# Second FFN's up projection by seven block products instead of eight (Strassen's scheme), with two of four weight sums made by accumulating DMAs

## Chip, core and metric

The kernel runs on one core of one Trainium2 chip. The metric is the device time of one launch in microseconds (us).

## What is computed

A decoder trunk of two layers works on 512 tokens of 1024 features in float32. Each layer adds a gated mixer (attention in layer 0, a state space layer beside a gated delta rule in layer 1) and then a gated convolutional feed-forward network (FFN). The change is in the second layer's FFN:

```python
def conv_ffn(h, w_up, conv_w, w_down):        # h 512 x 1024, w_up 1024 x 5632, w_down 2816 x 1024
    up = causal_dwconv(h @ w_up, conv_w)      # three taps over the tokens
    a, b = jnp.split(up, 2, axis=-1)          # 2816 columns each
    return (jax.nn.silu(a) * b) @ w_down
```

## The kernel before

Features lie on the 128 partitions and tokens on the free axis. Every float32 operand of a large product is split in two float32r tiles, the rounded value and the rest (`whi`, `wlo` for weights, `hh`, `hl` for activations), and a product of two operands is three matmuls: hi by hi, hi by lo, lo by hi (`mm3`, lines 324 to 326). One output tile of 128 features and 512 tokens takes eight feature blocks of the input, so 24 matmuls of 512 columns (`gemm`). A new stationary operand is loaded for every matmul.

`ffn` runs over `NJ` = 22 pairs of up-projection tiles, `j` for the half that passes through silu and `NJ + j` for the other. For pairs 0 and 1 (taken together, by halves of 256 tokens, right behind the norm) and then one pair at a time, it makes both products and calls `finish`: `conv` scales the accumulator on ScalarE (line 520) and adds two shifted copies on VectorE (lines 521, 522), for `a` and for `b`; then come silu (line 527), the product (line 529) and the split into `gh` and `gl` (lines 343, 344). Behind pairs 8 and 15 the down projection of the third that is complete is made (eight tiles, 24 or 21 matmuls each), and behind pair 21 the last third, in `out_gemm`.

Weights come by `prep`: SyncE loads a 128x1024 tile `st` of 512 KB, ScalarE rounds it (`whi`, line 312) and VectorE takes the rest (`wlo`, line 313). `weight` prepares `LA` = 2 tiles ahead. `st` has 2 buffers, `whi` and `wlo` have 5. The accumulators rotate over six PSUM banks named acc, s and o. `make_h` writes the normed activations: a scaled copy `hu` (line 474), then `hh` (line 475) and `hl` (line 476), by halves of 256 tokens. The order in which an engine meets its instructions is set at build time by a scheduler that goes by priorities, so instructions of neighbouring pairs interleave on each engine, while each engine works strictly through its own queue.

Of the kernel before, what the change touches and what calls it, by code (L numbers as in the profile page):

```python
# [8 lines left out]
F32 = mybir.dt.float32  # L9
F32R = mybir.dt.float32r  # L10
# [6 lines left out]
P = 128  # L17
T = 512
# [53 lines left out]
# features of the state space layer: groups of 16 (o) for states of odd and even tiles of states  # L72
# [3 lines left out]
def place(g):  # L76
    """Place of a group of 16 features among the eight of a half."""
    return 4 * (g // 2 % 2) + 2 * (g // 4) + g % 2
# [111 lines left out]
def weight_order():  # L190
    o = [("q", c, p) for p in range(2) for c in range(3)]
    o += [("q", c, p) for c in range(3, 9) for p in range(2)]
    o += [("wo", m) for m in range(8)]

    def ffn(l):
        r = []
        for j in range(NJ):
            r += [("up", l, j), ("up", l, NJ + j)]
            if j in THIRDS[1:3]:
                r += [("dn", l, THIRDS.index(j) - 1, m) for m in range(8)]  # L200
        return r + [("dn", l, 2, m) for m in range(8)]

    o += ffn(0)
    o += [("ri", 0), ("ri", 1), ("ab",)]
    kq = lambda p: [("ri", 8 + 2 * p), ("ri", 2 + 2 * p), ("ri", 9 + 2 * p), ("ri", 3 + 2 * p)]
    need = {"k": kq, "v": lambda p: [("ri", 14 + 2 * p), ("ri", 15 + 2 * p)], "z": lambda p: [("z", p, 0), ("z", p, 1)]}
    for e in SEQ.split():
        if e[0] in need:
            o += need[e[0]](int(e[1]))
    o += [("ro", m) for m in range(8)]  # L210
    o += ffn(1)
    return o
# [17 lines left out]
SPLIT_AT = (18, 18, 18, 18)  # L230
REC_K = (2, 3, 4, 5, 0, 1, 6, 7)


class Kernel:
    def __init__(self, nc, tc, I, O, ctx):
        self.nc, self.tc, self.I, self.O, self.ctx = nc, tc, I, O, ctx
        self.guards = {}
        self.cst = self.open("cst")
        self.wp = self.open("wp")
        self.sp = self.open("sp")  # L240
        self.ps = ctx.enter_context(tc.tile_pool(name="ps", bufs=1, space=PSUM))
        self.order = weight_order()
        self.index = {k: n for n, k in enumerate(self.order)}
        self.next = 0
        self.ready = {}
        self.LA = 2
        self.turn = 0
        self.tturn = 0

# [48 lines left out]

    def prep(self, pool=None, stage=None):
        key = self.order[self.next]  # L300
        self.next += 1
        src, n = self.source(key)
        nc = self.nc
        wp = pool or self.wp
        if stage:
            st = stage[0].tile([P, 1024], F32, name="ast", tag=stage[1], bufs=stage[2])[:, :n]
        else:
            st = wp.tile([P, 1024], F32, name="st", tag="st", bufs=1 if pool else 2)[:, :n]
        nc.sync.dma_start(st, src)
        hi = wp.tile([P, 1024], F32R, name="whi", tag="whi", bufs=1 if pool else 5)[:, :n]  # L310
        lo = wp.tile([P, 1024], F32R, name="wlo", tag="wlo", bufs=1 if pool else 5)[:, :n]
        nc.scalar.copy(hi, st)  # L312
        nc.vector.tensor_tensor(lo, st, hi.bitcast(F32), ALU.subtract)  # L313
        self.ready[key] = (hi, lo)

    def weight(self, key):
        ix = self.index[key]
        while self.next < min(ix + (self.LA if ix > 5 else 0) + 1, len(self.order)):
            self.prep()
        return self.ready.pop(key)  # L320
# [39 lines left out]
    def ada_first(self, k, pool, V):  # L360
        """Scale and shift of a feature tile of the first norm, in three steps: loads, long sums, last sums."""
# [11 lines left out]
        if k in ADA_PE:  # L373
            # four parts of the sum side by side on the tensor engine
# [67 lines left out]
    def rstd_bc(self, stats, cs, tag="x", warm=None):  # L442
        """1 / rms of each token, on all partitions; stats: squares to be summed."""
# [26 lines left out]
    def make_h(self, l, kind, k, rs, cs):  # L470
        nc = self.nc
        u = self.sp.tile([P, T], F32, name="hu", tag="hu", bufs=2)[:, cs]
        hi, lo = (t[:, cs] for t in self.h[k])
        nc.vector.scalar_tensor_tensor(u, self.x[k][:, cs], self.scale(l, kind, k), rs[:, cs], ALU.mult, ALU.mult)
        nc.scalar.activation(hi, u, AF.Identity, bias=self.shift(l, kind, k))  # L475
        self.last = nc.vector.scalar_tensor_tensor(lo, u, self.shift(l, kind, k), hi.bitcast(F32), ALU.add, ALU.subtract)  # L476
# [6 lines left out]
    def out_gemm(self, keys, rhs, gates, l, kind, hpool=None, order=None, tags=("acc", "acc", "s", "s", "o", "o", "acc", "acc")):  # L483
        """Products that end a half layer, with the norm that follows; the last tiles go by halves of the tokens."""
# [3 lines left out]
        for m0 in range(0, 4, 2):  # L488
            # the first two tiles leave the operand that comes last to the end
# [20 lines left out]
    def ffn(self, l, after, hpool=None):  # L510
        nc, tc = self.nc, self.tc
        lo, hi = slice(0, 256), slice(256, T)
        gp, tp = self.open(f"fg{l}", "right"), self.open(f"ft{l}", "right")
        if True:
            G = {}

            def conv(acc, c, tag):
                t = tp.tile([P, T], F32, name="t" + tag, tag="t" + tag, bufs=2)
# [18 lines left out]
            for j in range(NJ):  # L537
                if j < 2:
# [28 lines left out]
    def attention(self):  # L567
# [4 lines left out]
        if True:  # L572
# [13 lines left out]
            def rmsn(srcs, n):  # L586
                """Each head of both banks divided by its rms; srcs: [P, 2, n * 64] each."""
# [50 lines left out]
            def scores(pair, i, qT, kT, bias, isA):  # L638
                """Scores, softmax with its maximum, and division, for one block of queries of two heads."""
# [62 lines left out]
            # entry: modulation, norm and the first chunks together, feature tile by feature tile  # L702
# [3 lines left out]
            def keep_warm(n, k=0):  # L706
                """Products that nobody reads, to bring the tensor engine to its full clock and to keep it there."""
# [122 lines left out]
        # the turn of a state in two parts, the first short enough to be multiplied exactly  # L830
# [24 lines left out]
        # half angles keep the argument well inside the function's range  # L855
# [17 lines left out]
        # (l - 1) / lambda  # L873
# [67 lines left out]
    def s5_inputs(self):  # L941
        """W1, turned so that tokens and features of a chunk lie on the partitions."""
# [21 lines left out]
    def recurrent(self):  # L964
# [8 lines left out]
        # projections of u and of the decay and write rates; the first tiles by halves of the tokens  # L973
# [7 lines left out]
        # tokens of u by their place in a chunk  # L981
# [26 lines left out]
        # running sums of g with tokens on the free axis, rounded and rest on their own partitions, each chunk in its own columns  # L1008
# [70 lines left out]
        def decays(h):  # L1079
            """Of a head: exp(G) of every token, and exp(G_i - G_j) for the pairs of a chunk."""  # L1080
# [10 lines left out]
        def keys_queries(h, p):  # L1091
            """k and q of a head: decays, k's norm, and the two masked and decayed products with k."""
# [38 lines left out]
        def diagonal(p):  # L1131
            """Inverses of the 16 x 16 unit triangles on the diagonal, one to a partition, by substitution."""
# [29 lines left out]
        def block(flat, b):  # L1162
            """The 32 x 32 blocks b on the diagonals of all eight triangles, rows first."""
# [3 lines left out]
        def levels(p):  # L1167
            """Doubles the blocks of the inverses X and of their transposes W: the new block is -X22 N21 X11."""
# [8 lines left out]
            # 16 -> 32  # L1177
# [17 lines left out]
            # 32 -> 64  # L1195
# [18 lines left out]
            # 64 -> 128  # L1214
# [68 lines left out]
        def s5_load(f):  # L1283
            """What half of the features and of the states needs, the features' tokens by their place in a chunk."""
# [12 lines left out]
        def s5_states(f):  # L1297
            """States at the chunks' ends: the turn taken out, a real recurrence, the turn put back."""
# [31 lines left out]
        def s5_tokens(f):  # L1330
            """Outputs from the chunk's own tokens and from the state before it."""
# [21 lines left out]
        def s5_out():  # L1353
# [7 lines left out]
            for m in range(2):  # L1361
# [3 lines left out]
                # twice the gated output: 2 sigmoid(x) = 1 + tanh(x / 2), of the same table as gelu  # L1365
# [61 lines left out]
        hC = self.open("hC", "right")  # L1427
        self.out_gemm([("ro", m) for m in range(8)], rhs, lambda m: self.gate(1, 0, m), 1, 1, hC, REC_K, ("acc", "acc", "t", "x", "s", "s", "o", "o"))
# [91 lines left out]
```

## Time and profile before

| | |
|---|---|
| Runs of the kernel | 1324.92, 1325.09, 1325.41 us, median 1325.09 |
| Profiled execution: span from first to last instruction | 1321.6 us |
| Profiled execution: its own time | not recorded beside the span; the median of the runs is 3.5 us above the span |
| PE busy in the span | 1302.3 us (99%) |
| VectorE busy | 910.8 us (69%) |
| ScalarE busy | 576.0 us (44%) |
| Granted TensorE clock | 1.000 of full speed, mean |
| Matmuls | 8190 |

The profile names the engines PE (matmuls), PEld (loads of the stationary operand), DVE (VectorE), ACT (ScalarE), POOL (GpSimd) and SP (SyncE). A matmul's recorded duration overlaps its neighbours', and so does a VectorE instruction's; the distance from one start to the next tells what an engine can do. Times in a timeline count from the span's start. The second FFN's up projection begins at about 954 us with pairs 0 and 1.

### The profile page before, as it was taken

Reading aid. Unit: us, or ns where it says so; the run is one execution under the profiler, and the core shown is the slowest. Engines: PE = TensorE matmul, PEld = TensorE weight load, DVE = VectorE, ACT = ScalarE, POOL = GpSimd, SP = SyncE. Lnnn points to the kernel's source line nnn. Section 1 sums busy time; section 2 is a strip of 40 time slices with the busy share of each in tenths; the row PEclk is TensorE's granted clock in tenths of the full one; section 3 lists DMA queues with packets and bytes.
Section 4 is the critical chain, followed back from the end, with each engine's and each line's share of the span. In section 5 each row is a group of like instructions: output and inputs, shape, how many; then the busy total and the mean of one; then the engine's idle time right before and its main releaser. Section 6 shows DMA issues by size and latency. Waiting matters only on the chain.

```text
span 1321.6 us, 21082 instructions
## 1 busy us (share of the span) xinstructions
PE 1302.3 (99%) x8190; PEld 1075.0 (81%) x8190; DVE 910.8 (69%) x2025; ACT 576.0 (44%) x1114; POOL 3.3 (0%) x11
## 2 busy tenths in 40 slices
PE   8989999999999999999999999999999999999998
PEld 5976776898886888888998879787998888888888
DVE  6986856579995598486678786774885644654652
ACT  4456556445531333233456655553444423432430
POOL 0000000000000000000000000000000000000000
PEclk9999999999999999999999999999999999999999
DMA  9763521516654577363443522311422222222222
GB/s 365 267 224 119 175 65 41 201 65 217 213 170 154 178 252 248 125 212 116 142 159 100 156 92 63 98 31 59 150 97 98 96 96 97 95 94 101 94 79 78
DMA packets 81971, 181.02 MB, mean 137 GB/s; under 512 B 28432, under 2 KB 36048, under 8 KB 81872
## 3 DMA queue, kind: packets, MB, share of 16 engines
q1 hardware_dynamic: 81872, 179.69, 40.4%
q8 instruction: 64, 1.05, 0.3%
q14 instruction: 35, 0.29, 0.1%
HBM read 165.55 MB, written 14.11 MB: 136 GB/s over the span
## 4 chain that ended last, share of the span: by engine, by line
PE 91%; DVE 4%; DMA 2%; ACT 2%; issue 1%; SPq 0%; DVEq 0%; ACTq 0%
PE acc L324 12%; PE acc L325 12%; PE acc L326 12%; PE s L325 7%; PE s L324 7%; PE s L326 7%; PE o L325 7%; PE o L324 7%; PE o L326 6%; PE s L646 3%; PE o L675 2%; DMA ast<-ada 1%; DVE wlo L313 1%; DVE adaj L395 1%; PE t L666 1%
## 5 line engine op out<-in xcount | busy, mean ns | idle before, releaser
L312 ACT CAST whi<-st 128x1024 fp32r<-128x1024 f32 (+1 forms) x196 | 201.1, 1029 | 291.6 <-PE acc L325 101.9
L313 DVE TENSOR_TENSOR wlo<-st,whi 128x1024 fp32r<-128x1024 f32 (+1 forms) x196 | 234.1, 1196 | 127.3 <-ACT whi L312 124.7
L324 PE MATMUL acc<-hh,whi 128*128 128x512 f32 (+1 forms) x488 | 178.9, 370 | 0.9 <-ACT hh L475 0.7
L325 PE MATMUL acc<-hl,whi 128*128 128x512 f32 (+1 forms) x488 | 178.6, 369 | 0.2 <-DVE hl L344 0.2
L326 PE MATMUL acc<-hh,wlo 128*128 128x512 f32 (+1 forms) x488 | 178.0, 367 | 0.0
L325 PE MATMUL s<-hl,whi 128*128 128x512 f32 (+2 forms) x368 | 131.1, 356 | 0.0
L324 PE MATMUL s<-hh,whi 128*128 128x512 f32 (+2 forms) x368 | 130.3, 354 | 0.0
L326 PE MATMUL s<-hh,wlo 128*128 128x512 f32 (+2 forms) x368 | 129.9, 353 | 0.0
L395 DVE CUSTOM_DVE_ANT_0 adaj<-ast,cond 128x1024 bf16<-128x1024 f32 x86 | 104.8, 1218 | 13.8 <-DMA ast<-ada 13.5
L325 PE MATMUL o<-hl,whi 128*128 128x512 f32 (+1 forms) x288 | 106.8, 371 | 0.0
L324 PE MATMUL o<-hh,whi 128*128 128x512 f32 (+1 forms) x288 | 106.7, 370 | 0.0
L326 PE MATMUL o<-hh,wlo 128*128 128x512 f32 (+1 forms) x288 | 106.1, 368 | 0.0
L324 PEld LDWEIGHTS acc<-hh,whi 128*128 128x128 f32 x488 | 91.1, 188 | 17.0 <-ACT hh L475 1.0
L325 PEld LDWEIGHTS acc<-hl,whi 128*128 128x128 f32 x488 | 91.3, 188 | 16.2 <-DVE hl L344 1.2
L326 PEld LDWEIGHTS acc<-hh,wlo 128*128 128x128 f32 x488 | 91.4, 188 | 15.2 <-issue 0.7
L325 PE MATMUL acc<-wlo,hh 128*128 128x256 f32 x320 | 93.3, 292 | 0.0
L324 PE MATMUL acc<-whi,hh 128*128 128x256 f32 x320 | 92.5, 290 | 0.6 <-ACT hh L475 0.6
L326 PE MATMUL acc<-whi,hl 128*128 128x256 f32 x320 | 91.6, 288 | 0.9 <-DVE hl L476 0.9
L324 PEld LDWEIGHTS s<-hh,whi 128*128 128x128 f32 (+1 forms) x368 | 68.3, 186 | 10.8
L326 PEld LDWEIGHTS s<-hh,wlo 128*128 128x128 f32 (+1 forms) x368 | 68.3, 186 | 10.4
L325 PEld LDWEIGHTS s<-hl,whi 128*128 128x128 f32 (+1 forms) x368 | 68.3, 186 | 9.9
L324 PEld LDWEIGHTS acc<-whi,hh 128*128 128x128 f32 x320 | 60.4, 189 | 4.9 <-issue 3.2
(439 smaller groups left out, 2593.5 us busy)
## 6 DMA issues: line engine op xcount, KB each, us to landing
ast<-ada SPq DMA_DIRECT2D x92, 512.0 KB
st<-up SPq DMA_DIRECT2D x88, 512.0 KB
st<-dn SPq DMA_DIRECT2D x32, 448.0 KB
st<-ri SPq DMA_DIRECT2D x20, 512.0 KB
st<-wq SPq DMA_DIRECT2D x17, 512.0 KB
st<-dn SPq DMA_DIRECT2D x16, 512.0 KB
st<-wo SPq DMA_DIRECT2D x8, 512.0 KB
st<-ro SPq DMA_DIRECT2D x8, 512.0 KB
```

The lines of the kernel that those rows point to most:

```text
L312: nc.scalar.copy(hi, st)
L313: nc.vector.tensor_tensor(lo, st, hi.bitcast(F32), ALU.subtract)
L324: mm(out, lh, rh, start=start, stop=False)
L325: mm(out, lh, rl, start=False, stop=False)
L326: mm(out, ll, rh, start=False, stop=stop)
L395: self.nc.vector.tensor_tensor_reduce(junk, st, self.cond, 1.0, 0.0, op0=ALU.mult, op1=ALU.add, accum_out=self.md[l][:, i:i + 1])
L646: nc.tensor.matmul(sb, qT[pr, i * P:(i + 1) * P], kT[pr, j0 * P:(i + 1) * P], start=True, stop=True)
L666: nc.tensor.transpose(tb[:, j * P:(j + 1) * P], ps[par][:, j * P:(j + 1) * P], self.ident)
L675: nc.tensor.matmul(ob[64 * par:64 * par + 64, i * P:(i + 1) * P], V[:, j0 + j, vc:vc + 64], pts[:, par, j * P:(j + 1) * P], start=j == 0, ...
```

## The change

Pairs 2 to 21 of the second FFN are no longer made tile by tile. Let A11 and A12 be the two halves of tile `j` (input features 0 to 511 and 512 to 1023), A21 and A22 those of tile `NJ + j`, and B11, B12, B21, B22 the activations by halves of the features (first index) and of the tokens (second index). The seven products are of 128 output features, 512 input features and 256 tokens, so 12 matmuls of 256 columns each: 84 for a pair, where there were 48 of 512 columns. Weight factors beside A11, A12 and A22 are S3 = A11 + A21, S1 = A21 + A22, S2 = A11 + S1 and S4 = A12 + S2.

- `prep_pair` loads A11 and A12 as one 128x1024 tile `a`, A11 (from tile `j`) and A22 (from tile `NJ + j`) as the halves `b1` and `b2` of a second tile. After A22 is split, GpSimd issues two DMAs that add A21 from HBM onto `b1` and `b2`. VectorE then adds `b2` to the first half of `a`, and that to its second half. The seven factors are split: three casts and subtractions of 1024 columns and one of 512, where there were two of 1024. A pair is prepared one pair ahead; odd pairs take their `st` buffers from another pool.
- `token_sums` makes, once, the four sums of activations from copies `hk` that `make_h` now keeps, and splits them.
- `seven` makes the products in the order A11, S3, S2, A22, S1, A12, S4 in three banks of 256 columns, Z, X and Y. Z and X take further products on top of earlier ones, and partial sums are copied out on the way: three copies (`p1`, `p7`, `p16`) and one (`ua`) by ScalarE, three combinations by VectorE. The convolution then reads `ua` and `ub` from SBUF instead of PSUM.

```diff
@@ weight_order
-            r += [("up", l, j), ("up", l, NJ + j)]
+            r += [("sp", l, j)] if l in FAST and j >= PLAIN else [("up", l, j), ("up", l, NJ + j)]
+FAST = (1,)
+PLAIN = 2
+SUMS = "VV"
+    def prep_pair(self, l, j):
+        nc = self.nc
+        pool = (self.wp, self.fp)[j % 2]
+        a, b = (pool.tile([P, 1024], F32, name="st", tag="st", bufs=2) for _ in range(2))
+        nc.sync.dma_start(a, self.I["up"][l, j])
+        b1, b2 = b[:, :T], b[:, T:]
+        nc.sync.dma_start(b1, self.I["up"][l, j, :, :T])
+        nc.sync.dma_start(b2, self.I["up"][l, NJ + j, :, T:])
+        def halves(src, pool, tag, bufs):
+            n = src.shape[1]
+            hi, lo = (pool.tile([P, n], F32R, name=tag + e, tag=tag + e, bufs=bufs) for e in ("hi", "lo"))
+            nc.scalar.copy(hi, src)
+            nc.vector.tensor_tensor(lo, src, hi.bitcast(F32), ALU.subtract)
+            return [(hi[:, c:c + T], lo[:, c:c + T]) for c in range(0, n, T)]
+        f = {}
+        f["11"], f["12"] = halves(a, self.wp, "w", 5)
+        f["22"], = halves(b[:, T:], self.fp, "v", 2)
+        eng = [nc.vector if e == "V" else nc.gpsimd for e in SUMS]
+        a1, a2 = a[:, :T], a[:, T:]
+        for d in (b1, b2):
+            nc.gpsimd.dma_start(d, self.I["up"][l, NJ + j, :, :T], accum_op=ALU.add)
+        eng[0].tensor_tensor(a1, a1, b2, ALU.add)
+        f["s3"], f["s1"] = halves(b, self.wp, "w", 5)
+        eng[1].tensor_tensor(a2, a2, a1, ALU.add)
+        f["s2"], f["s4"] = halves(a, self.wp, "w", 5)
+        return f
@@ weight
-        while self.next < min(ix + (self.LA if ix > 5 else 0) + 1, len(self.order)):
+        ahead = (1 if key[0] == "sp" else self.LA) if ix > 5 else 0
+        while self.next < min(ix + ahead + 1, len(self.order)):
@@ make_h
+            if k not in self.keep:
+                self.keep[k] = self.keep_pool.tile([P, T], F32, name="hk", tag="gh", bufs=10)
+            u = self.keep[k][:, cs]
+    def token_sums(self, l, tp):
...
+        for k in range(KD):
+            h = self.keep[k]
+            nc.scalar.activation(h, h, AF.Identity, bias=self.shift(l, 1, k))
+        for k in range(4):
+            h, g = self.keep[k], self.keep[k + 4]
...
+            V_.tensor_tensor(a, h[:, t1], h[:, t2], ALU.subtract)
+            V_.tensor_tensor(c, g[:, t2], h[:, t2], ALU.subtract)
+            V_.scalar_tensor_tensor(b, a, -1.0, g[:, t2], ALU.mult, ALU.subtract)
+            V_.scalar_tensor_tensor(d, b, -1.0, g[:, t1], ALU.mult, ALU.subtract)
+            for e, (n, m) in enumerate((("1", "3"), ("2", "4"))):
+                hi, lo = self.split(s[e], *(tp.tile([P, T], F32R, name=f"b{k}{e}{x}") for x in "hl"))
...
+    def seven(self, f, B, tp):
+        Z, X, Y = (self.gbank()[:, t1] for _ in range(3))
+        u, v = (tp.tile([P, T], F32, name=n, tag=n, bufs=1) for n in ("ua", "ub"))
+        def product(acc, a, b, start):
+            for k in range(4):
+                s = slice(k * P, (k + 1) * P)
+                (lh, ll), (rh, rl) = f[a], B[b][k]
+                for n, (x, y) in enumerate(((lh, rh), (lh, rl), (ll, rh))):
+                    nc.tensor.matmul(acc, x[:, s], y, start=start and k == n == 0, stop=k == 3 and n == 2, skip_group_check=not start)
...
+        product(Z, "11", "11", True)
+        p1 = keep(Z, "p1")
+        product(X, "s3", "3", True)
+        p7 = keep(X, "p7")
+        product(Z, "s2", "2", False)
+        p16 = keep(Z, "p16")
+        product(X, "22", "4", False)
+        V_.scalar_tensor_tensor(v[:, t1], X, -1.0, p16, ALU.mult, ALU.subtract)
+        product(Z, "s1", "1", False)
+        V_.scalar_tensor_tensor(v[:, t2], Z, -1.0, p7, ALU.mult, ALU.subtract)
+        product(Y, "12", "21", True)
+        V_.tensor_tensor(u[:, t1], Y, p1, ALU.add)
+        product(Z, "s4", "22", False)
+        S_.copy(u[:, t2], Z)
+        return u, v
@@ ffn
+        nb = 1 if fast else 2
...
-                t = tp.tile([P, T], F32, name="t" + tag, tag="t" + tag, bufs=2)
+                t = tp.tile([P, T], F32, name="t" + tag, tag="t" + tag, bufs=nb)
...
-                if j < 2:
+                if fast and j >= PLAIN:
+                    aa, bb = self.seven(self.weight(("sp", l, j)), B, tp)
+                elif j < 2:
```

How the change moves instructions stands below for two engines. Lines in rows of the changed kernel are its own: 319 is `wlo` and `vlo` of `halves`, 329 and 331 are the two sums by VectorE, 596 is a matmul of `product`, 610, 612 and 614 are the three combinations in `seven` (612 reads Z behind the fifth product), 637 and 638 the convolution, 645 the product with silu, 384 the split's rest. The number behind a name tells buffers apart.

VectorE, middle of the second FFN, one pair, before:

```order
L529 TENSOR_TENSOR tb_11497<-ta_11492,tb_11497 128x512
L344 TENSOR_TENSOR gl_11503<-tb_11497,gh_11502 128x512
L313 TENSOR_TENSOR wlo_11617<-st_11614,whi_11616 128x1024
L521 SCALAR_TENSOR_TENSOR ta_11568<-acc_11506,pc_70,ta_11568 128x511
L522 SCALAR_TENSOR_TENSOR ta_11568<-acc_11506,pc_70,ta_11568 128x510
L313 TENSOR_TENSOR wlo_11662<-st_11659,whi_11661 128x1024
L521 SCALAR_TENSOR_TENSOR tb_11573<-acc_11537,pc_70,tb_11573 128x511
L522 SCALAR_TENSOR_TENSOR tb_11573<-acc_11537,pc_70,tb_11573 128x510
```

VectorE at the same place now, from the combination of pair 10 that reads Z on through twelve of a pair's fifteen instructions (`st_12133` and `st_12134` are pair 12's, `st_11995` pair 11's):

```order
L612 SCALAR_TENSOR_TENSOR ub_12024<-acc_12020,p7_12051 128x256
L319 TENSOR_TENSOR wlo_12017<-st_11995,whi_12016 128x1024
L614 TENSOR_TENSOR ua_12023<-s_12022,p1_12037 128x256
L637 SCALAR_TENSOR_TENSOR tb_12124<-ub_12024,pc_70,tb_12124 128x511
L319 TENSOR_TENSOR wlo_12139<-st_12133,whi_12138 128x1024
L638 SCALAR_TENSOR_TENSOR tb_12124<-ub_12024,pc_70,tb_12124 128x510
L637 SCALAR_TENSOR_TENSOR ta_12119<-ua_12023,pc_70,ta_12119 128x511
L329 TENSOR_TENSOR st_12133<-st_12133,st_12134 128x512
L638 SCALAR_TENSOR_TENSOR ta_12119<-ua_12023,pc_70,ta_12119 128x510
L319 TENSOR_TENSOR wlo_12150<-st_12134,whi_12149 128x1024
L645 TENSOR_TENSOR tb_12124<-ta_12119,tb_12124 128x512
L331 TENSOR_TENSOR st_12133<-st_12133 128x512
```

Eight instructions for a pair have become fifteen: those twelve, and behind them 610, 384 and a `vlo` of 512 columns before the next 612. The weights of pair 12 are made among the ends of pair 10. From pair 9 on the PE works through each pair's seven products in the program's order.

The PE at the first pair by seven products (pair 2: `o_10660` is Z, `o_10661` X, `acc_10662` Y), now:

```order
L596 MATMUL o_10660<-hh3_10086,wlo_10392 128x256
L596 MATMUL acc_10662<-hh4_10088,whi_10391 128x256
L596 MATMUL o_10661<-b00h_10324,whi_10402 128x256
L596 MATMUL o_10661<-b00l_10325,whi_10402 128x256
L596 MATMUL acc_10662<-hl4_10089,whi_10391 128x256
L596 MATMUL acc_10662<-hh4_10088,wlo_10392 128x256
L596 MATMUL acc_10662<-hh5_10090,whi_10391 128x256
L596 MATMUL acc_10662<-hl5_10091,whi_10391 128x256
L596 MATMUL o_10661<-b00h_10324,wlo_10403 128x256
```

In pairs 2 to 8 products are broken up and mixed: parts of the sixth product (Y) stand between parts of the second (X), and matmuls of the next pair's first product stand before the last ones of a pair.

## Rows read from the trace of the kernel before

**Rows 1.** Page, part 1: busy time, share of the span and instructions of engines.
```profile
PE 1302.3 (99%) x8190; PEld 1075.0 (81%) x8190; DVE 910.8 (69%) x2025; ACT 576.0 (44%) x1114; POOL 3.3 (0%) x11
```
**Rows 2.** Windows: stretch, then busy us of PE, PEld, DVE, ACT, POOL; clock; DMA share, GB/s.
```profile
300.00:333.00 33.00, 33.00 (x152) 26.96 (x151) 31.13 (x47) 16.43 (x22) 0.00 (x0) 1.00 0.70 228
333.00:366.00 33.00, 33.00 (x143) 26.59 (x142) 32.51 (x68) 19.05 (x27) 0.00 (x0) 1.00 0.64 217
366.00:400.00 34.00, 34.00 (x148) 27.45 (x147) 32.79 (x59) 11.56 (x17) 0.00 (x0) 1.00 0.54 177
1232.00:1243.00 11.00, 11.00 (x49) 9.01 (x48) 6.67 (x9) 4.53 (x6) 0.00 (x0) 1.00 0.26 95
```
**Rows 3.** Timeline, PE: start us, us; where pairs 2 and 3 and down projections start.
```profile
976.81 0.39 PE L324 MATMUL o<-hh,whi 128*128 128x512 f32 x1
987.79 0.39 PE L324 MATMUL acc<-hh,whi 128*128 128x512 f32 x1
...
1053.71 0.39 PE L324 MATMUL acc<-gh,whi 128*128 128x512 f32 x1
...
1097.66 0.39 PE L324 MATMUL s<-hh,whi 128*128 128x512 f32 x1
...
1174.57 0.39 PE L324 MATMUL o<-gh,whi 128*128 128x512 f32 x1
```
**Rows 4.** Timeline, PE, end of the kernel: matmuls of 256 columns, 117 steps apart.
```profile
1303.11 0.28 PE L324 MATMUL acc<-gh,whi 128*128 128x256 f32 x1
...
1316.89 0.28 PE L324 MATMUL acc<-gh,whi 128*128 128x256 f32 x1
```
**Rows 5.** Timeline, DVE, first FFN: instructions back to back.
```profile
299.80 0.74 DVE L522 SCALAR_TENSOR_TENSOR tb<-acc,pc,tb 128x510 f32<-128x510 f32 x1
300.46 0.74 DVE L521 SCALAR_TENSOR_TENSOR ta<-s,pc,ta 128x511 f32<-128x511 f32 x1
301.12 1.21 DVE L313 TENSOR_TENSOR wlo<-st,whi 128x1024 fp32r<-128x1024 f32 x1
302.25 0.68 DVE L529 TENSOR_TENSOR tb<-ta,tb 128x512 f32<-128x512 f32 x1
302.85 0.74 DVE L522 SCALAR_TENSOR_TENSOR ta<-s,pc,ta 128x510 f32<-128x510 f32 x1
```
**Rows 6.** Groups by form, DVE: line, operation, tiles, shapes, count, busy us, mean ns.
```profile
L1370 DVE SCALAR_TENSOR_TENSOR uT<-gate,uT 128x512 f32<-128x512 f32 x2 | 1.4, 692 | 0.3 <-PE x L1364 0.3
```
**Rows 7.** Timeline, DVE, before the second FFN: instructions of 256 columns back to back.
```profile
953.46 0.41 DVE L437 TENSOR_TENSOR stat<-stat,sq 128x256 f32<-128x256 f32 x1
953.79 0.47 DVE L429 SCALAR_TENSOR_TENSOR x<-o,mb,x 128x256 f32<-128x256 f32 x1
954.18 1.21 DVE L313 TENSOR_TENSOR wlo<-st,whi 128x1024 fp32r<-128x1024 f32 x1
```
**Rows 8.** Timeline, DVE: start of the norm's second half of the tokens.
```profile
962.44 0.87 DVE L474 SCALAR_TENSOR_TENSOR hu<-x,am,t 128x256 f32<-128x256 f32 x2 [0.87 <-PE t L460]
```
**Rows 9.** Groups by form, ACT: casts of weights, and copies of 256 columns from PSUM.
```profile
L312 ACT CAST whi<-st 128x1024 fp32r<-128x1024 f32 x163 | 170.5, 1048 | 234.8 <-PE acc L325 80.0 <-PE s L325 73.1 <-PE o L325 46.9
L667 ACT COPY PT<-x 128x256 f32<-128x256 f32 x16 | 6.0, 373 | 5.7 <-PE x L666 5.5
```
**Rows 10.** Timeline, start of the kernel: SP's loads of 256 KB, and the first user.
```profile
1.18 3.73 SPq L1456 DMA_DIRECT2D x<-xt  x8
4.04 0.63 ACT L713 ACTIVATE stat<-x 128x512 f32<-128x512 f32 x1 [2.02 <-DMA x<-xt]
```

More of the change, by code (lines that the diff above doesn't have):

```diff
@@ L236, in __init__ @@
         self.nc, self.tc, self.I, self.O, self.ctx = nc, tc, I, O, ctx
-        self.guards = {}
+        self.guards, self.guarded = {}, {}
         self.cst = self.open("cst")
@@ L248, in __init__ @@
         self.tturn = 0
+        self.keep = None
     def open(self, name, side="left"):
@@ L254, in open @@
         self.guards[name] = p
+        self.guarded[name] = t
         return t
@@ L301, in prep @@
         self.next += 1
+        if key[0] == "sp":
+            self.ready[key] = self.prep_pair(*key[1:])
+            return
         src, n = self.source(key)
@@ L471, in make_h @@
         nc = self.nc
-        u = self.sp.tile([P, T], F32, name="hu", tag="hu", bufs=2)[:, cs]
+        if self.keep is None:
+            u = self.sp.tile([P, T], F32, name="hu", tag="hu", bufs=2)[:, cs]
+        else:
+            if k not in self.keep:
+                self.keep[k] = self.keep_pool.tile([P, T], F32, name="hk", tag="gh", bufs=10)
+            u = self.keep[k][:, cs]
         hi, lo = (t[:, cs] for t in self.h[k])
@@ L507, in out_gemm @@
                 self.norm(l, kind, stat, cs)
+    def token_sums(self, l, tp):
+        nc = self.nc
+        t1, t2 = slice(0, 256), slice(256, T)
+        V_ = nc.vector
+        B = {n: [] for n in ("11", "21", "22", "1", "2", "3", "4")}
+        for k in range(KD):
[3 more added lines that the diff above has]
+            h, g = self.keep[k], self.keep[k + 4]
+            s = [self.keep_pool.tile([P, T], F32, name="ts", tag="gl", bufs=10) for _ in range(2)]
+            a, c, b, d = s[0][:, t1], s[0][:, t2], s[1][:, t1], s[1][:, t2]
+            V_.tensor_tensor(a, h[:, t1], h[:, t2], ALU.subtract)
[4 more added lines that the diff above has]
+                hi, lo = self.split(s[e], *(tp.tile([P, T], F32R, name=f"b{k}{e}{x}") for x in "hl"))
+                B[n].append((hi[:, t1], lo[:, t1]))
+                B[m].append((hi[:, t2], lo[:, t2]))
+            for n, q, t in (("11", k, t1), ("21", k + 4, t1), ("22", k + 4, t2)):
+                B[n].append(tuple(v[:, t] for v in self.h[q]))
+        self.keep = None
+        return B
@@ new lines, in seven, with keep @@
+    def seven(self, f, B, tp):
+        nc = self.nc
+        V_, S_ = nc.vector, nc.scalar
+        t1, t2 = slice(0, 256), slice(256, T)
+        Z, X, Y = (self.gbank()[:, t1] for _ in range(3))
[6 more added lines that the diff above has]
+                    nc.tensor.matmul(acc, x[:, s], y, start=start and k == n == 0, stop=k == 3 and n == 2, skip_group_check=not start)
+        def keep(acc, nm):
+            t = tp.tile([P, 256], F32, name=nm, tag=nm, bufs=2 if nm == "p1" else 1)
+            S_.copy(t, acc)
+            return t
+        product(Z, "11", "11", True)
[13 more added lines that the diff above has]
+        return u, v
@@ L512, in ffn @@
         lo, hi = slice(0, 256), slice(256, T)
-        gp, tp = self.open(f"fg{l}", "right"), self.open(f"ft{l}", "right")
+        fast = l in FAST
+        if not fast:
+            self.open(f"fg{l}", "right")
+        gp, tp = self.guarded[f"fg{l}"], self.open(f"ft{l}", "right")
+        nb = 1 if fast else 2
         if True:
             G = {}
+            if fast:
+                self.fp = tp
+                B = self.token_sums(l, tp)
             def conv(acc, c, tag):
-                t = tp.tile([P, T], F32, name="t" + tag, tag="t" + tag, bufs=2)
+                t = tp.tile([P, T], F32, name="t" + tag, tag="t" + tag, bufs=nb)
                 o = 132 * l + 3 * c
@@ L1427, in recurrent @@
         hC = self.open("hC", "right")
+        self.keep, self.keep_pool = {}, self.open("fg1", "right")
         self.out_gemm([("ro", m) for m in range(8)], rhs, lambda m: self.gate(1, 0, m), 1, 1, hC, REC_K, ("acc", "acc", "t", "x", "s", "s", "o", "o"))
```

## Prediction

> **What bounds the kernel now.** I read the page's first part first: PE is busy for 99% of the span, DVE for 69%, ACT for 44% [rows 1]. PE sets the time as a whole. The windows say whether the other engines have room in the stage that changes: in one pair's 11 us DVE works 6.67 and ACT 4.53 us, and PE never stops [rows 2]. The timeline gives the pace: pair 3 starts 10.98 us after pair 2, which over 48 matmuls is 0.2288 us each, and the seven pairs between the down projections take 1174.57 - 1097.66 = 76.9 us, again 10.99 each [rows 3]. So a pair costs what its matmuls cost.
>
> Busy time is not what an engine can carry, since neighbours overlap. Back to back, DVE's instructions of 512 columns start 0.60 us apart, two reading an accumulator in PSUM 0.66, one of 1024 columns keeps the next away 1.13 [rows 5]; with 256 columns it is 0.33 from SBUF and 0.39 from PSUM [rows 7]. An SBUF-only scalar_tensor_tensor of 512 columns lasts 692 ns [rows 6], like the product whose successor starts 0.60 later, so I count 0.60 for it. I price with distances from start to start (1.14, 0.60, 0.40, 0.34).
>
> **The change, part by part.**
>
> *PE.* Matmuls of 256 columns at the kernel's end run 13.78 us over 117 steps, 0.1178 each [rows 4]. A pair was 48 x 0.2288 = 10.99 and becomes 84 x 0.1178 = 9.89. If PE stays the bound, 20 pairs save 22 us. A product of 12 takes 1.41.
>
> *DVE.* A pair had two `wlo` and six others of 512 columns, 6.67 us. Now: three `wlo` 3.42, `vlo` 0.60, two sums 1.20, three combinations of 256 columns 1.20, four taps 2.40 (their source has moved to SBUF), the product with silu 0.60, the rest of the split 0.60. Together **10.02 us, more than PE's 9.89**. DVE becomes the bound. How full can it be? In the first FFN, over 100 us, it was busy 31.13, 32.51 and 32.79 of 33, 33 and 34 us, 96.4% [rows 2]. PE was never idle there either, so this is what DVE has carried, not its ceiling; but here it must also wait for products and copies, so I take it: 10.02 / 0.964 = 10.39 us a pair. Bounds: 98.5% (the best of the three windows) gives 10.17, 94.3% (the worst) 10.63.
>
> *ACT.* At most two casts more (1.05 each) and four copies of 256 columns (0.37 each) [rows 9]: 4.53 + 2.10 + 1.49 = 8.1 of 10.4 us. It stays under DVE, which hides it. A copy that holds up a bank of PE has a product's 1.41 us (another bank's) to be done in; 0.37 fits.
>
> *DMA.* SP's loads stay 1 MB a pair (three instead of two), with 0.5 MB of accumulating DMAs on POOL: the queues' share of 0.26 [rows 2] becomes about 0.4. POOL has 3.3 us of other work in the whole kernel [rows 1], and nothing else queues behind its 40 DMAs. The first accumulation waits only for a load, early. The second, onto `b2`, waits for `vlo`, and the sum of line 329 waits for it; between those two stand seven to eight of DVE's instructions, 4.6 to 5.1 us. The nearest row is a plain 256 KB load at the start, used 2.9 us after its issue [rows 10]. I take the accumulation as hidden. Lower bound 2.9, upper bound open: what is later than the budget stops DVE in line 329, with the taps and the next pair's weights queued behind, and PE for them, and costs its lateness in every pair.
>
> *Start.* DVE has its queue to clear, from the norm's second half at 962.44 [rows 8] to line 612 of pair 8: by the new order 22 of 1024 columns (25.1), 45 tensor_tensors of 512 (27.0), 32 taps (16 of them from PSUM, 19.7), 35 of 256 columns (14.0) and the 16 token sums (5.4), in all 91.2 us. At 96.4% that is 94.6, so 612 is done at 1057.0. The last product behind it adds 1.41; about 0.9 us of the down projection's matmuls already lie in PE's gaps. The down projection is then at its full start at 1057.5, against 1053.71 [rows 3]: **+3.8**. Mixing pairs 2 to 8 on PE gives no time of its own, because PE has slack there: its seven pairs take 69.2 us of the 80 from 976.8 [rows 3] on.
>
> *Pairs 9 to 15.* During the down projection DVE gets ahead, so pair 9 runs at PE's pace: five products 7.06 us, and 0.5 (estimate) till 612 is through. From there 612 repeats every 10.39, six times, and the last product takes 1.41: 7.6 + 62.3 + 1.4 = 71.3 against 76.9: **-5.6**.
>
> *Pairs 16 to 21.* 7.6 + 5 x 10.39 + 1.4 = 61.0 against 6 x 10.99 = 65.9: **-4.9**. Pair 21's finish, about 5 us, has some 36 matmuls of the last third (8.2 us) beside it: 0, at most +1.
>
> Sum: 3.8 - 5.6 - 4.9 = -6.7. The profiled span of 1321.6 becomes 1314.9; the median of the runs lies 3.5 above the span, so 1325.1 becomes 1318.4, which I round to **1318**. At 98.5% the same three terms give 1314.0, at 94.3% 1323.2. A tenth of a us on a pair's period is 2 us on the end (11 whole periods, and about 9 periods' worth of DVE work at the start).
>
> [...]
>
> **The rivals.**
>
> A. *PE is the bound after all, and the start is hidden*: 22 us less, 1303. For: 10.02 and 9.89 differ by 1%. Against: DVE would have to run at 100% and clear 91 us of queue in the first stage.
>
> B. *DVE loses its overlap* (slower). Each instruction then pays its whole duration, since many now wait for a neighbour on ACT or PE (cast to `wlo`, copy to combination) instead of standing ready. Durations: three of 1.21, five of 0.68, four taps of 0.69, three of 0.47 [rows 5 to 7], 11.2 us a pair. Against 10.39 that is 20.1 x 0.82 = 16 us more: 1334.8. It decides from a period of 10.7 on, where the gain is gone. For: fifteen instructions hang on three engines, and a pair is prepared only one ahead. Against: over 100 us in the first FFN the share held at 96%. [...]
>
> C. *The second accumulating DMA lands late* (slower). Each us beyond the budget costs about 19 us. The gain is gone when it takes some 5.3 us; at 6.0 us the time is near 1339. For: it must read what it adds to, and POOL must issue it. Against: 2.9 us for a plain load leaves about 2. [...]
>
> **How the numbers follow.** Forecast 0.60, A 0.06, B 0.17, C 0.17. A measurement of this kernel can tell about 0.2%, 2.65 us, from no change: faster is below 1322.4, slower above 1327.7. Within the forecast most values lie below 1322.4 (0.47), some between (0.10), a few above (0.03). A adds 0.06 to faster; B and C, where they hold only in part, add 0.03 to faster and 0.05 to no change, and the rest, 0.26, to slower. Faster 0.56, same 0.15, slower 0.29. Both signs have weight; the forecast alone lies between 1311 and 1325. The range goes to 1336, taking in B and the milder half of C, and starts at 1309, just under a DVE at 100% (10.02 a pair, 1310.9); A and late cases of C stay out.
>
> **What would show it.** In the changed profile: matmuls of line 596 start 0.118 apart where they don't wait; line 612 repeats every 10.4 us between the down projections; DVE is 95% busy or more there and PE idle for about half a us a pair, on DVE; the first down projection starts about 4 us later than before, the stretches of pairs 9 to 15 and 16 to 21 are some 5 us shorter each. A shows as PE without gaps at 9.9 a pair. B shows as DVE starts farther apart than 0.60 and 1.13 at a period near 11.2, with idle time ended by ACT or PE. C shows as line 329 idle behind a DMA of POOL that lands over 5 us after `vlo`. I am wrong if a term is: a granted clock below 1.00, a matmul of 256 columns above 0.118 because its weight load is no longer covered, or a wait on copies that takes DVE below 94%.

## The result, and the profile after

The changed kernel takes 1349.45 us (median of 4 runs, 1347.62 to 1349.97), the kernel before 1325.01 on the same chip: a ratio of **1.0187**, interval 1.0175 to 1.0199 (the two medians alone give 1.0184). It is slower by 24 us, where 7 us faster was forecast. The profiled execution took 1349.12 us, its span is 1347.4.

Page of the changed kernel, part 1, to be read beside [rows 1]:

```profile
PE 1295.1 (96%) x8910; PEld 1101.6 (82%) x8910; DVE 995.6 (74%) x2189; ACT 641.6 (48%) x1250; POOL 38.1 (3%) x51
```

PE is busy for 7.2 us less than before, where 22 were promised. It now stands still for 4% of a longer span, and no other engine comes near 100%. Where it stands still is told by the first matmuls of pairs 9 and 16 in PE's timeline (compare [rows 3]; pair 16 began at 1213.02 before):

```profile
1111.65 0.28 PE L596 MATMUL s<-hh,whi 128*128 128x256 f32 x1
...
1234.95 0.28 PE L596 MATMUL s<-hh,whi 128*128 128x256 f32 x1
```

These two starts cut the span in three stages that I use for all kernels below: everything up to pair 9; pairs 9 to 15 with the second down projection; pair 16 to the end.

| us | to pair 9 | pair 9 to 16 | 16 to the end | span |
|---|---|---|---|---|
| before | 1097.7 | 115.4 | 108.6 | 1321.6 |
| forecast | 1101.5 | 109.7 | 103.7 | 1314.9 |
| after | 1111.7 | 123.3 | 112.4 | 1347.4 |

All three missed, by 10, 14 and 9 us. What PE waits for from pair 9 to pair 21 (waits of PE, changed kernel: engine, tile and line, what it waited for, us in total, times, longest):

```profile
PE acc L596 <- ACT p L600: 7.9, 3, 3.6
PE s L596 <- ACT p L600: 7.0, 4, 3.0
PE o L596 <- ACT p L600: 3.5, 2, 2.6
PE acc L596 <- DVE ub L612: 0.2, 1, 0.2
PE o L596 <- DVE ub L612: 0.2, 1, 0.2
```

18.4 us, in nine waits, for ScalarE's copies of a partial sum, 0.4 for VectorE. All nine stand in front of the third product (S2), which adds onto the bank that the copy `p1` reads. But a copy takes 0.37 us; it was late because of what stood ahead of it. ScalarE's timeline around the longest of these waits:

```profile
1171.26 0.72 ACT L636 ACTIVATE ta<-ua,pc 128x512 f32<-128x512 f32 x1
1175.81 1.04 ACT L318 CAST whi<-st 128x1024 fp32r<-128x1024 f32 x1 [3.83 <-DMA st<-up]
1176.76 0.64 ACT L600 COPY p<-acc 128x256 f32<-128x256 f32 x2
```

The cast of `b` (line 318, the next pair's S3 and S1) waits 3.83 us for a DMA, and the copies `p1` and `p7` stand behind it in ScalarE's queue. The DMA is the second accumulating one. It was issued late, and it was slow. POOL's and VectorE's timelines of the same place:

```profile
1169.98 0.86 POOL L328 DMA_DIRECT2D st<-up  x1 [7.58 <-ACT tb L636]
```
```profile
1168.43 0.42 DVE L612 SCALAR_TENSOR_TENSOR ub<-s,p 128x256 f32<-128x256 f32 x1
1168.77 0.68 DVE L319 TENSOR_TENSOR vlo<-st,vhi 128x512 fp32r<-128x512 f32 x1
...
1172.63 0.74 DVE L637 SCALAR_TENSOR_TENSOR ta<-ua,pc,ta 128x511 f32<-128x511 f32 x1
1173.29 0.74 DVE L638 SCALAR_TENSOR_TENSOR tb<-ub,pc,tb 128x510 f32<-128x510 f32 x1
...
1175.76 0.69 DVE L329 TENSOR_TENSOR st<-st 128x512 f32<-128x512 f32 x1 [1.06 <-DMA st<-up]
```

`vlo` starts at 1168.77, the accumulation (which waits for it and for ScalarE's reading of `b2`) is issued at 1169.98 and has landed at 1175.7, 7.0 us after `vlo` began. VectorE meets the wait too, in line 329, but only for the last 1.06 us; ScalarE's cast had its turn 2.7 us sooner. And the chain of waits shows that this closes a circle (start, us, what):

```profile
1143.17 5.15 DMA st<-up
...
1148.39 0.09 ACT whi L318
1148.48 0.86 issue
1149.34 0.38 ACT p L600
1149.72 0.04 issue
1149.76 4.38 PE acc L596 x35
1154.14 0.02 issue
1154.16 0.88 ACT whi L318
...
1155.13 0.71 ACT tb L636
1155.85 0.28 issue
1156.12 4.56 DMA st<-up
```

DMA, cast of `b`, copy, three products of PE, line 612, which reads the last of them, `vlo` right behind it in VectorE's queue, DMA again: from issue to issue 1156.12 - 1143.17 = 12.95 us, where PE needs 9.89. (The chain names line 636 on ScalarE as the last step, because it ended last before the issue. But the issue follows the end of `vlo` by 0.53 us at 1143.17, 1156.12 and 1169.98 alike, so `vlo` is the one waited for.) Over all 40 accumulating DMAs, landing, from the issue until the data is in place, took this long (source of line 328):

```profile
DMA to landing us min/median/max: 3.6/4.0/6.0
```

Last, the granted clock (windows of the changed kernel; columns as in [rows 2]):

```profile
984.00:988.00 4.00, 2.05 (x8) 1.79 (x9) 2.62 (x4) 1.58 (x2) 0.00 (x0) 0.57 0.65 106
988.00:992.00 4.00, 4.00 (x23) 4.00 (x23) 3.90 (x6) 3.73 (x5) 0.00 (x0) 0.58 0.38 139
1112.00:1197.00 85.00, 73.92 (x590) 72.64 (x589) 64.72 (x95) 47.95 (x79) 8.65 (x10) 0.94 0.45 116
```

After an idle stretch of 4.4 us (4.37, ended at 984.49) PE gets 0.57 and 0.58 of its clock in these two windows, over eight us. Over pairs 9 to 15 the mean is 0.94; the matmuls there keep PE busy for 73.92 us where 590 x 0.1178 = 69.5 were due.

### The profile page after: what moved, and what is told of

It is laid out like the page before. It is cut to its first block, busy times and chain, and to the rows that moved or that the text cites. A ratio compares the mean times of both kernels' runs of the same rounds, so it can differ in the third digit from the quotient of the medians.

```text
span 1347.4 us, 23028 instructions
## 1 busy us (share of the span) xinstructions
PE 1295.1 (96%) x8910; PEld 1101.6 (82%) x8910; DVE 995.6 (74%) x2189; ACT 641.6 (48%) x1250; POOL 38.1 (3%) x51
## 3 DMA queue, kind: packets, MB, share of 16 engines
q8 instruction: 70, 1.15, 0.4%
## 5 line engine op out<-in xcount | busy, mean ns | idle before, releaser
L351 ACT CAST whi<-st 128x1024 fp32r<-128x1024 f32 (+1 forms) x156 | 159.2, 1024 | 214.8 <-PE acc L365 69.7
L352 DVE TENSOR_TENSOR wlo<-st,whi 128x1024 fp32r<-128x1024 f32 (+1 forms) x156 | 185.1, 1189 | 52.3 <-ACT whi L351 50.4
L318 ACT CAST whi<-st 128x1024 fp32r<-128x1024 f32 x60 | 62.2, 1046 | 89.8 <-DMA st<-up 40.8
L365 PE MATMUL s<-hl,whi 128*128 128x512 f32 (+2 forms) x256 | 86.8, 339 | 0.0
L364 PE MATMUL s<-hh,whi 128*128 128x512 f32 (+2 forms) x256 | 86.4, 338 | 0.0
L366 PE MATMUL s<-hh,wlo 128*128 128x512 f32 (+2 forms) x256 | 86.4, 338 | 0.0
L366 PEld LDWEIGHTS acc<-hh,wlo 128*128 128x128 f32 x392 | 73.4, 188 | 11.2 <-issue 0.7
L319 DVE TENSOR_TENSOR wlo<-st,whi 128x1024 fp32r<-128x1024 f32 x60 | 73.0, 1220 | 9.7 <-ACT whi L318 8.8
L366 PE MATMUL acc<-gh,wlo 128*128 128x512 f32 (+1 forms) x182 | 65.1, 357 | 0.0
L365 PE MATMUL acc<-gl,whi 128*128 128x512 f32 (+1 forms) x182 | 65.0, 357 | 0.0
L364 PE MATMUL acc<-gh,whi 128*128 128x512 f32 (+1 forms) x182 | 64.7, 356 | 0.0
L365 PEld LDWEIGHTS acc<-wlo,hh 128*128 128x128 f32 x320 | 61.5, 192 | 3.9 <-issue 3.7
```

Of the source, the lines that this page charges most:

```text
L318: nc.scalar.copy(hi, src)
L319: nc.vector.tensor_tensor(lo, src, hi.bitcast(F32), ALU.subtract)
L364: mm(out, lh, rh, start=start, stop=False)
L365: mm(out, lh, rl, start=False, stop=False)
L366: mm(out, ll, rh, start=False, stop=stop)
```

## Experiments

Theory 1 after this reading: the second accumulating DMA lands too late, a queue (ScalarE's) stands behind it, and PE behind the queue. Rival 2: VectorE, at 10.0 us of work a pair, or with its overlap lost, sets the pace, and the waits only show where.

| us, one profiled execution | to pair 9 | pair 9 to 16 | 16 to the end | span |
|---|---|---|---|---|
| e1, no accumulation | 1104.8 | 107.6 | 101.2 | 1313.7 |
| e2, A22 loaded twice | 1105.2 | 109.8 | 102.3 | 1317.3 |
| e3, cast behind `p16` | 1112.1 | 118.5 | 108.7 | 1339.3 |
| e4, from pair 9 | 1096.8 | 123.5 | 109.8 | 1330.1 |
| e5, every second pair | 1104.6 | 110.6 | 104.0 | 1319.2 |
| e6, as e2, from pair 4 | 1103.3 | 111.1 | 103.0 | 1317.4 |
| e7, sums by VectorE | 1113.4 | 109.7 | 103.2 | 1326.3 |
| e8, as e2 and e5 | 1108.7 | 110.0 | 104.3 | 1322.9 |
| e9, as e7, from pair 9 | 1099.0 | 109.5 | 102.9 | 1311.4 |
| e10, as e2, from pair 9 | 1101.1 | 110.4 | 103.2 | 1314.7 |
| e11, as e7, from pair 6 | 1099.8 | 109.5 | 103.4 | 1312.6 |
| e12, as e9, pairs 5 and 7 too | 1096.7 | 109.7 | 102.9 | 1309.3 |

### e1: no accumulating DMAs

```diff
-        for d in (b1, b2):
-            nc.gpsimd.dma_start(d, self.I["up"][l, NJ + j, :, :T], accum_op=ALU.add)
```

> Leaves the 40 accumulating DMAs out (so S3 and S1 are not the sums they should be); every other instruction of the changed kernel stays. Theory 1: ScalarE's cast of b stands in its queue ahead of the copies p1, p7, p16, waits up to 4 us for the second accumulating DMA, and PE waits for the copies. Then the waits go: pairs 9 to 15 take about 71 us instead of 84.9, pairs 16 to 21 about 61 instead of 70.3, pair 9 starts near 1102 to 1107, and the time is about 1318 to 1323. Rival 2: VectorE's work or its lost overlap sets the pace; its work is the same, so pairs 9 to 15 stay above 80 us and the time stays above 1340.

Measured: 1314.74 us, ratio 0.992 (0.9897 to 0.9943). Rival 2 falls, and the time is below even theory 1's range. Windows of this kernel, the first two at the start of pair 2, the next two in the middle of pairs 9 to 15, the last all seven pairs:

```profile
980.00:985.00 5.00, 2.00 (x18) 1.80 (x16) 5.00 (x9) 1.56 (x4) 0.00 (x0) 1.00 0.00 0
985.00:1000.00 15.00, 13.93 (x89) 13.14 (x90) 13.35 (x20) 8.51 (x13) 0.00 (x0) 0.77 0.42 141
```
```profile
1120.00:1140.00 20.00, 19.87 (x172) 19.67 (x172) 20.00 (x30) 15.16 (x25) 0.00 (x0) 1.00 0.32 107
1140.00:1160.00 20.00, 19.96 (x169) 19.58 (x169) 20.00 (x31) 14.75 (x24) 0.00 (x0) 1.00 0.29 99
1105.00:1174.00 69.00, 68.83 (x588) 68.06 (x588) 63.11 (x94) 48.46 (x78) 0.00 (x0) 1.00 0.32 104
```

From pair 9 on PE is the bound: its 588 matmuls are done in 69 us, 9.88 a pair, the price by [rows 4]. VectorE is busy for 40.00 of 40 us in the middle and still holds PE up for next to nothing. It is not faster than PE, though. The counterpart of line 612, which is line 610 in e1, repeats every 10.05 us there, the time of VectorE's fifteen instructions back to back (VectorE's timeline, e1):

```profile
1132.10 0.42 DVE L610 SCALAR_TENSOR_TENSOR ub<-s,p 128x256 f32<-128x256 f32 x1
...
1142.15 0.42 DVE L610 SCALAR_TENSOR_TENSOR ub<-acc,p 128x256 f32<-128x256 f32 x1
```

So VectorE falls 0.17 us a pair behind PE, 1.2 us in seven pairs, and its lead covers that: PE is idle for 0.17 us of the 69. A longer stretch was not run. What is left of the loss lies at the start: VectorE is at work without a break while PE idles (5.00 and 2.00 of 5 us), and then the clock is at 0.77 for 15 us.

Against the changed kernel e1 is 33.7 us shorter in span: 6.8 up to pair 9, 15.7 from 9 to 16, 11.2 behind. That is what the 40 accumulations cost.

### e2: the same sums, but nothing ahead of the accumulation

```diff
+        c = self.sp.tile([P, T], F32, name="sc", tag="hu", bufs=2)
+        nc.sync.dma_start(c, self.I["up"][l, NJ + j, :, T:])
...
-        f["22"], = halves(b[:, T:], self.fp, "v", 2)
+        f["22"], = halves(c, self.fp, "v", 2)
```

> A22 is loaded a second time into a tile of its own for the split, so neither accumulating DMA waits for vlo, only for loads. Theory 1: both land before ScalarE meets the cast; pairs 9 to 15 take 71 to 75 us, pairs 16 to 21 61 to 64, the time is 1318 to 1328, though four loads a pair could cost a little. If it is the landing of loads and not the wait for vlo that makes the accumulations late, the time stays above 1335. Rival 2 (VectorE sets the pace): no change, above 1340.

Measured: 1320.31 us, ratio 0.9965 (0.9952 to 0.9979); pairs 9 to 15 in 71.4 us, 16 to 21 in 59.6. As theory 1 says: with the accumulation no longer behind `vlo`, 29 us come back. From pair 9 on 3.3 us remain against e1. The landing itself is slower here, where the accumulations are issued in pairs beside four loads (source of the accumulations, e2), so ScalarE's cast still waits now and then, 11.6 us in five waits:

```profile
DMA to landing us min/median/max: 3.6/5.3/7.9
```

### e3: the cast moved behind the copies

```diff
-        f["s3"], f["s1"] = halves(b, self.wp, "w", 5)
-        eng[1].tensor_tensor(a2, a2, a1, ALU.add)
-        f["s2"], f["s4"] = halves(a, self.wp, "w", 5)
+        def late():
+            f["s3"], f["s1"] = halves(b, self.wp, "w", 5)
+            eng[1].tensor_tensor(a2, a2, a1, ALU.add)
+            f["s2"], f["s4"] = halves(a, self.wp, "w", 5)
+        self.late.append(late)
...
@@ seven, behind p16 = keep(Z, "p16")
+        if self.late:
+            with self.tc.issue_after(self.pk.ins):
+                self.late.pop()()
...
```

> The same DMAs and the same work; only the casts of b and of the second sums, with what hangs on them, are written behind the copy p16 of the pair before, in ScalarE's queue. Theory 1: the accumulations land as late as before but nobody behind the cast waits; pairs 9 to 15 take 71 to 76 us, pairs 16 to 21 61 to 65, the time is 1318 to 1330. Rival 2: above 1340.

Measured: 1344.05 us, ratio 1.0146 (1.012 to 1.0171). This miss teaches most. PE's waits for `p` are all but gone, and another has taken their place (waits of PE, then of VectorE, in pairs 9 to 15):

```profile
PE s L601 <- DVE ub L620: 4.0, 2, 2.4
PE acc L601 <- DVE ub L620: 2.1, 1, 2.1
PE acc L601 <- ACT p L605: 0.7, 1, 0.7
```
```profile
DVE st L330 <- DMA st<-up: 6.5, 3, 2.4
DVE wlo L320 <- ACT whi L319: 6.2, 5, 4.7
```

VectorE's first sum (line 330 here) waits for the same DMA, with the combination that PE needs (line 620, the 612 of the change) behind it. VectorE also waits for the moved casts themselves, but the longest of those waits, at 1117.7, has no wait of PE behind it. So it is not ScalarE's place that costs, but that whoever waits has PE's next step behind it. Theory 1 stands with this correction: taking one queue out of the wait passes it to the next.

### e4: seven products from pair 9 on

```diff
-PLAIN = 2
+PLAIN = 9
```

> Seven products only from pair 9 on; pairs 2 to 8 are made as before the change, the token sums lie beside them. Both theories: pairs 9 to 15 and 16 to 21 take 84.9 and 70.3 us as in the changed kernel; pair 9 starts at 1098 to 1100 instead of 1111.7, so the time is 1335 to 1338. If the start loses more than the sums and pairs 2 to 8 (a clock that stays lower later), it is below 1335.

Measured: 1340.85 us (1331.92 to 1341.77; the profiled execution is the fastest), ratio 1.0104 (1.0066 to 1.0142), somewhat above what was expected. Pair 9 starts at 1096.8, so the token sums beside plain pairs cost nothing; from pair 9 to 16 it takes 123.5 us, as in the changed kernel.

### e7: no accumulating DMA, all sums by VectorE

```diff
+        c = self.sp.tile([P, T], F32, name="sc", tag="hu", bufs=2)
...
+        nc.sync.dma_start(c, self.I["up"][l, NJ + j, :, :T])
...
-            nc.gpsimd.dma_start(d, self.I["up"][l, NJ + j, :, :T], accum_op=ALU.add)
+            nc.vector.tensor_tensor(d, d, c, ALU.add)
```

> All four weight sums by VectorE from a plain load of A21, no accumulating DMA. VectorE has 1.2 us more a pair: 11.2 us by distances from start to start. If VectorE then sets the pace at close to its whole time: pairs 9 to 15 take about 76 us, pairs 16 to 21 about 65, pair 9 starts near 1110, the time is 1334 to 1342. Rival (PE is still the bound, as in e1): pairs 9 to 15 take 69 to 71 us and the time is 1314 to 1322.

Measured: 1328.36 us, ratio 1.0018 (1.0002 to 1.0034). Each side is right in its stage. Up to pair 9 the time fits VectorE's queue: 8.5 us more than e1, near the 9.6 of 16 additions of 0.60. From pair 9 on PE is the bound, though VectorE has 11.2 us of work a pair: PE waits for 0.8 us in all of pairs 9 to 21 (waits of PE, e7):

```profile
PE o L598 <- ACT whi L320: 0.8, 1, 0.8
```

Those stages are short, and the weights of their first two pairs are made during the down projection, when VectorE has room: in 31 us of it, it is busy for 20 (windows of the changed kernel):

```profile
1067.00:1098.00 31.00, 31.00 (x142) 25.64 (x142) 19.99 (x25) 12.31 (x15) 1.73 (x2) 1.00 0.46 137
```

### e5, e8, e6: fewer pairs, or a later start

e5 makes pairs 3, 5, ... 21 by seven products, e8 does so with e2's second load, e6 is e2 from pair 4 on. In e5 and e8 `weight` also prepares two tiles ahead again, unless the pair is followed by another by seven products (not shown).

```diff
+SEVENS = range(3, 22, 2)
...
-                if fast and j >= PLAIN:
+                if fast and j in SEVENS:
```

> Only every second pair (3, 5, ... 21) by seven products, with the change's own accumulating DMAs; the ten others as before the change. Theory 1 (an accumulation that lands 4 us after vlo holds a queue, and PE for it): a pair has twice the time to be prepared, so the waits shrink or go; ten pairs save 1.1 us each: 1313 to 1317; if each still waits as long as in the changed kernel (1 to 2 us), 1325 to 1335. Rival 2 (VectorE): its work per two pairs is 16 of 20.9 us, so it gives 1314 too.

Measured: 1318.29 us, ratio 0.9948 (0.9922 to 0.9973). From pair 9 to 16 it takes 110.6 us: four pairs at 9.89, three at 10.99 and the down projection's 38.45 would be 111.0. With twice the time for a pair, the change's own accumulations are hidden: PE is busy for 120.00 of the 120 us from 1100 on. The start is not. A load lands late there, `vhi` waits for it on ScalarE, the copies stand behind, and PE waits 4.0 us for one of them at 1040.3 (ScalarE's timeline, e5):

```profile
1037.34 0.62 ACT L319 CAST vhi<-st 128x512 fp32r<-128x512 f32 x1 [3.66 <-DMA st<-up]
```

> Every second pair by seven products as in e5, and A22 loaded twice as in e2. Theory 1: no wait is left; ten pairs save 1.1 us each, the start is covered: 1312 to 1316, and not more than 2 us below e5 unless the accumulations were still late there.

Measured: 1324.91 us, ratio 0.999 (0.9973 to 1.0006). Missed, by the start alone (pair 9 at 1108.7). ScalarE's timeline has a cast that waits 6.20 us there, for two accumulations that POOL had issued together at 1000.61:

```profile
1008.41 1.05 ACT L321 CAST whi<-st 128x1024 fp32r<-128x1024 f32 x1 [6.20 <-DMA st<-up]
```

But PE's own waits up to pair 9 come to 6.5 us in e8 and 5.7 in e5, so they do not explain why e8 gets to pair 9 4.1 us later. That stays open.

> The version with A22 loaded twice (e2), and pairs 2 and 3 as before the change, so that the token sums and the first weights have 22 us more. If the start's 7.5 us in e2 are VectorE's queue of sums and preparations at one place: pair 9 starts at 1098 to 1101 instead of 1105.2, the rest as in e2, the time is 1314 to 1317. If they are a price of pairs 4 to 8 as such: 1320 or more.

Measured: 1318.4 us, ratio 0.994 (0.9916 to 0.9963); pair 9 at 1103.3. Two plain pairs hide only part of the start.

### e9 to e12: versions that beat both kernels

e9 and e11 are e7 with PLAIN = 9 and 6, e10 is e2 with PLAIN = 9, e12 is e9 with pairs 5 and 7 by seven products as well (and with e5's `weight`).

> All four weight sums by VectorE (as e7), seven products only from pair 9 on (as e4). If the start's loss is VectorE's queue of token sums, splits and weights in pairs 2 to 8, and nothing waits on an accumulation: pair 9 starts near 1097, pairs 9 to 15 take 69.5 to 71.5 us, pairs 16 to 21 59 to 61, the time is 1309 to 1314. If VectorE's 11.2 us a pair is the bound where no backlog of e7's kind precedes: pairs 9 to 15 take 76, 16 to 21 65 us, the time is 1321 to 1326.

Measured: 1313.7 us, ratio 0.9916 (0.9901 to 0.9931).

> A22 loaded twice (as e2), seven products only from pair 9 on (as e4): pair 9 starts near 1097, then 71.5 and 59.6 us as in e2, the time is 1309 to 1315. Against e9 it tells what the accumulating DMAs still cost when they wait for loads alone: 1 to 3 us.

Measured: 1315.83 us, ratio 0.9939 (0.9919 to 0.9959).

> As e9, with seven products from pair 6 on. If VectorE's queue has been cleared during the four plain pairs: three more pairs save 1.1 us each, 1306 to 1311. If pairs 6 to 8, right after one another, run into VectorE's bound of 11.2 us: the same as e9 or up to 2 us above.

Measured: **1311.81 us**, ratio 0.9902 (0.9887 to 0.9917).

> As e9, with pairs 5 and 7 by seven products too (6 and 8 plain): VectorE has 17.3 of 20.9 us there. Two pairs more save 2.2 us: 1307 to 1312.

Measured: 1312.08 us, ratio 0.9907 (0.9892 to 0.9921).

e9 lies in its range, e10 to e12 end 0.1 to 0.8 us above theirs. e10, which keeps the accumulating DMAs, is 2.1 us above e9, but their intervals overlap. With no accumulating DMA between two of VectorE's instructions, and the start left to plain pairs, the seven products are worth about 1% of the kernel. The intervals of e9, e11 and e12 overlap, so which of them is best stays open.

## Why the prediction was wrong

- **PE: 9.89 us a pair, right.** e1's pairs 9 to 15 take 9.88 each. A pair's matmuls do what they promise once nothing holds them up.
- **"I take the accumulation as hidden": the step that failed.** I bounded the landing from below by a plain load, 2.9 us [rows 10], left the other end open, and chose the lower one. It measured 3.6 to 6.0 us, and with the issue behind `vlo` 7.0 in the place shown. The three stages owe it 33.7 us (e1). Without the accumulations the kernel takes 1314.7 us, near the forecast, and that is partly luck: the start is 3.3 us slower than forecast there, the two later stages are 4.7 us faster.
- **Who waits.** I gave the wait a budget of 4.6 to 5.1 us up to VectorE's line 329 and checked only that engine. The cast of line 318 reads the same tile, on ScalarE, where its turn comes about 3 us after `vlo`. "It stays under DVE, which hides it" was said of busy time; a queue that is 48% busy held PE up for 18.4 us in pairs 9 to 21: in the place shown its copies stood behind a cast that waited 3.83 us. Rival C (0.17) is what came true, but on another engine; e3, whose span is 25.6 us above e1's, shows that on VectorE it costs most of that too. C's price fits only loosely: at 19 us for a us of lateness, 33.7 us are 1.8 us beyond the budget of 4.9, so a landing 6.7 us after the start of `vlo`; behind the `vlo` of pairs 11 to 15 and 18 to 21 it was 4.7 to 7.0, in the median 5.7. POOL's issue took 0.86 us in the median and 1.15 at most.
- **"DVE becomes the bound": wrong from pair 9 on.** A pair's work, 10.02 us by my sum, measures 10.05 in e1, but by luck: taps that read SBUF start 0.66 us apart (1172.63, 1173.29 above), not 0.60, and combinations of 256 columns 0.34 (1168.43, 1168.77), not 0.40. What failed is the share and the spreading. In the rows I took for its limit PE was saturated, as I noted, so 96.4% was no measure of what VectorE can carry; in e1 it runs 40.00 of 40 us. And I spread the whole work of a pair over each pair of a stage, though two pairs are made ahead. Rival A's pace (0.06) is the true one there: -7.8 and -7.4 us in e1 where I had -5.6 and -4.9.
- **The start: +3.8 forecast, +7.1 in e1.** The sum of VectorE's work held nearly, its place did not. VectorE's timeline in e1, the norm's second half and line 610, the counterpart of 612, of pair 8:

```profile
965.51 0.86 DVE L517 SCALAR_TENSOR_TENSOR hk<-x,am,t 128x256 f32<-128x256 f32 x2
...
1061.17 0.42 DVE L610 SCALAR_TENSOR_TENSOR ub<-o,p 128x256 f32<-128x256 f32 x1
```

  That is 96.1 us to its end, for my 94.6, but from 965.51 and not from 962.44 [rows 8], so it is done at 1061.6, against 1057.0. (In the sum, 19.7 us for the taps is the figure for eight of them from PSUM, as there are, and not for the sixteen I wrote.) I also missed that PE idles early, when the token sums stand ahead of the first weights, and loses time to the clock afterwards (0.77 for 15 us, 3.4 us). How much of the 3.3 us each of the two is worth no run separates. In the changed kernel accumulations add 6.8.
- **Rival B, lost overlap: not seen.** Starts lie as far apart as before in VectorE's timeline of the changed kernel, 1.14 us behind a `wlo` of 1024 columns, where it was 1.13 [rows 5]:

```profile
1122.09 1.22 DVE L319 TENSOR_TENSOR wlo<-st,whi 128x1024 fp32r<-128x1024 f32 x1
1123.23 0.74 DVE L638 SCALAR_TENSOR_TENSOR tb<-ub,pc,tb 128x510 f32<-128x510 f32 x1
```

  In e1 a pair's fifteen instructions take 10.05 us, and not the 11.2 that B adds up from whole durations.
- **The clock** was counted at 1.00. It fell behind some of PE's gaps, and made them dearer: of pairs 9 to 15, 11 us were idle and some 4 to 5 us slower matmuls (an estimate: 73.92 us busy for 69.5 due), at a mean clock of 0.94.
- **The step from span to time**, 3.5 us, joined two different executions. Where one execution has both, it is 1.7 to 2.1 us.

What stays open: how much of the 4.0 us landing is the adding onto the target, how much POOL's issue (0.86 us each) and how much the traffic beside it. No run separates them.

## What to carry to other kernels

Work that was moved from an engine to a DMA between two steps of a tile's preparation was paid for here in latency (3.6 to 6.0 us to land), not in throughput (a DMA share of 0.45 in pairs 9 to 15). So list every instruction on every engine that reads the tile, find what PE needs behind each of them in its queue, and compare the landing with the earliest. When a price is open at one end, ask what the time would be at the dear end before choosing the cheap one. And put new set-up work where an engine has slack, not ahead of the first weights.

## What was not expected of the hardware

- VectorE kept going at 40.00 busy us of 40, at 10.05 us a pair, without slowing PE's 9.88 (e1).
- An accumulating DMA of 256 KB took 3.6 to 6.0 us to land, 5.3 in the median and up to 7.9 with two issued in a row beside four loads (e2), where a plain one was used after 2.9 [rows 10].
- The granted clock fell to 0.57 after an idle gap of 4.4 us. But the length of the gap alone does not tell: after one of 3.15 us, ended at 1149.76, it stayed at 1.00, and after one of 2.46 us, ended at 1162.14, it was at 0.50 (windows of the changed kernel):

```profile
1149.70:1153.70 4.00, 3.94 (x33) 3.94 (x34) 2.62 (x4) 2.09 (x6) 0.28 (x1) 1.00 0.67 166
1162.10:1165.10 3.00, 2.96 (x14) 2.97 (x15) 2.17 (x3) 0.79 (x2) 0.30 (x1) 0.50 0.57 99
```
